# A hybrid attention and expert block on one core: the queries' and keys' projections moved ahead of the linear attention's

## The chip, the cores and the metric

The kernel runs as one launch on one core of a Trainium2 chip. The metric is the device time of the launch in microseconds. Before the change it is 1333.85 us, the median of three runs (1331.14 to 1338.91). The engines are TensorE (PE, its weight loads as PEld), VectorE (DVE), ScalarE (ACT), GpSimd (POOL) and SyncE (SP), which only issues DMAs here.

## The reference, cut to what matters

The block works on 1024 tokens of width 1024.

```
proj = h @ w_in
aq, ak, av, iq, ik, iw, bq, bk, bv, br, bg = split(proj)
aq, ak, iq, ik = rope(...)                      # rotary embedding
ya = dsa_mixer(aq, ak, av, iq, ik, iw)          # 8 heads of 64; each query sees the 256
                                                # admitted keys with the best index score
yb = gla_mixer(bq, bk, bv, log_a)               # gated linear attention, 4 heads, chunks of 64
yb = rms_norm(yb) * g_gla_norm * silu(br)
h  = layer_norm(alpha * h + concat(ya, yb) @ w_out)
y  = layer_norm(alpha * h + hier_moe(h))        # 32 experts, 2 for each token
```

In `dsa_mixer` the index score of a query and a key is `sum over 8 heads of iw * relu(iq . ik)`, keys of later chunks are excluded, and the top 256 are taken with ties in order of index. In `gla_mixer` the decay is a cumulative sum over a chunk of `log_sigmoid(bg @ w_gla_gate + b) / 16`, and the state passes from chunk to chunk.

## The kernel before, in words

Matrix products with large weights are done in a shorter format (fp32r) with both operands split in a high and a low part, and three products are summed: high x high, low x high, high x low. `proj_t` (L214 to L224) projects 128 output columns for 512 tokens with 24 matmuls of 128x512, `proj_n` (L226 to L238) two tiles of 128 tokens for 256 columns with 48 matmuls of 128x256. The splits are a cast (L179, ACT) and a subtraction (L180, DVE or POOL).

The stages around the change, in the order of the program:

- Index queries, keys and scores, beside the values' projections. Then `rest_inputs`: the second half of the values and all six projections of the linear attention (`gla_inputs`, L498: for each of two head pairs hp, k=0 the queries and keys, k=1 the values, k=2 the gate). All of it goes to DRAM.
- `queries_keys` (L657): four weight blocks of 256 columns, each projected for both halves of the tokens; rope is four DVE products from PSUM (L264 to L267) and two POOL sums (L268, L269); the result is split (ACT L179, POOL L180) and written to `d_q` and `d_k` in DRAM.
- `topk_phase` (L676): for each of six tiles of 128 queries the threshold of the 256 best is found by bisection over the bits of the score. In each of 31 bits DVE counts four tiles (L689) and ACT two (L719, by an accumulated Sign), and small DVE instructions on 128x2 or 128x4 turn counts into the next candidate (L715, L722, L723). Then come the masks, tile by tile (L738 to L750): `gt` (above the threshold, DVE L743), `eq` (equal, DVE L744), the count of `gt` (ACT L745), a running count of `eq` (DVE scan L746), the number still needed (L747), the ties taken (L748), a POOL sum (L749) and the additive bias (L750), which lies over the scores.
- `gla_phase` (L523): the linear attention in four halves (2 head pairs x 2 halves of the tokens, `gla_half`, L540), under high priority.
- `attention` (L776): 4 head pairs x 8 tiles of queries = 32 items, in three steps a turn apart: scores (L795, PE), the maximum (L800, DVE) and the exponential (L808, ACT); the transposes (L819) and their copies (L822 DVE, L824 ACT); the product with the values (`mixed`, L833). After every fourth item of a pair the reciprocal of the sums is spread by POOL (`rb`, L878), transposed into `pt` (L841), multiplied into `R` (L843) and stored in `d_mix` (`shares`). The order of PE, ACT and DVE in this stage is as written; POOL and SP are not part of that.
- `before(n)` (L334) is called ahead of item n. It loads the operands of the next pairs; at n = 8 it closes the pool `first_qk` of the first pair's operands, and in the place that is free then opens the pools of the split output weights, `wlo` and `whi` (1024x1024 each); from there on 16 pieces of w_out are loaded (`woraw`, two buffers, L901) and split by POOL into `wohi` (L908) and `wolo` (L909).
- `out_phase`: the mixed heads come back from `d_mix` into `mraw`, which has the two buffers of `woraw` (one tag, L977, L979); they are split, and multiplied by `wohi` and `wolo` (L997). Then layer norm, routing, and the 32 experts.

Outside the attention the order is the tile scheduler's: it goes by program order and priority, and an instruction that writes a buffer waits for the last readers of what lay there before. Of PSUM the linear attention has two banks (`g`) and the projections six (`acc`), all given up before the attention's (`s` two double ones, `pt` two, `ot` two) are opened.

Of the kernel before, what the change touches and what calls it, by code (L numbers as in the profile page):

```python
# [8 lines left out]
F32 = mybir.dt.float32  # L9
# [10 lines left out]
T = 1024  # L20
D = 1024
# [78 lines left out]
def const_block():  # L100
# [17 lines left out]
    add("tri", causal / 16.0)  # L118
# [10 lines left out]
NCONST = CONST_COLS["tri"][0]  # L129
# [34 lines left out]
class Kern:  # L164
# [85 lines left out]
    def banks(self, ctx, name, **tags):  # L250

        pool = ctx.enter_context(self.pool(name, space=PSUM))
        for t, n in tags.items():
            self.kinds[t] = (pool, n)

    def bank(self, kind, shape):
        pool, n = self.kinds[kind]
        return pool.tile(shape, F32, name=kind, bufs=n)
# [24 lines left out]
    def run(self):  # L283
        tc, nc, I = self.tc, self.nc, self.I
        with ExitStack() as ctx:
# [28 lines left out]
            with ExitStack() as ps:  # L314
                self.banks(ps, "psg", g=2)
                with ExitStack() as p1:
                    self.banks(p1, "ps1", acc=6)
                    self.in_phase(gla)
            self.rp = ctx.enter_context(self.pool("route"))
            with ExitStack() as ps:  # L320
                self.banks(ps, "ps2", s=2, pt=2, ot=2)
                gla.close()
                oc = outc.enter_context(self.pool("outc"))
                with self.pool("att") as ap:

                    first = ExitStack()
                    fq = first.enter_context(self.pool("first_qk", side="right"))
                    loads = [self.attention_loads(0, [fq.tile([128, 2, D], F32R, name=f"kq{i}") for i in range(3)] + [self.big()])]
# [5 lines left out]
                    def before(n):  # L334
# [31 lines left out]
    def in_phase(self, gla):  # L366
        tc, nc, I = self.tc, self.nc, self.I
        with ExitStack() as ctx:
# [6 lines left out]
            with self.pool("first") as fp:  # L375
                cI = fp.tile([128, T], F32, name="cI")
                sI = fp.tile([128, T], F32, name="sI")
                with self.pool("xraw") as xr:
# [14 lines left out]
                    K2 = self.wpool.tile([128, NCONST2], F32, name="Kin")  # L393
                    nc.sync.dma_start(K2, I["const"][:, NCONST:])
                    self.c.update({n: K2[:, a - NCONST:b - NCONST] for n, (a, b) in CONST_COLS.items() if a >= NCONST})
                    nc.gpsimd.tensor_copy(self.ones, self.c["ones"])
                    nc.gpsimd.tensor_copy(self.before, self.c["before"])
# [100 lines left out]
    def gla_inputs(self, gg):  # L498

        nc, I = self.nc, self.I  # L500
        for hp in range(2):
            w = self.load_w(I["wi"][P_GLA + 3 * hp], 256)
# [6 lines left out]
            w = self.load_w(I["wi"][P_GLA + 3 * hp + 1], 256)  # L509
# [5 lines left out]
            w = self.load_w(I["wi"][P_GLA + 3 * hp + 2], 256)  # L515
# [7 lines left out]
    def gla_phase(self, p):  # L523
# [6 lines left out]
        causal = p.tile([128, 128], I32, name="causal")  # L530
        nc.vector.tensor_copy(causal, self.c["causal"])
# [8 lines left out]
    def gla_half(self, p, hp, h, S, wg, AT, causal):  # L540
# [25 lines left out]
        for i in range(4):  # L566
            nc.tensor.matmul(bp[:, 128 * i:128 * i + 128], loga[:, 128 * i:128 * i + 128], self.c["tri"],
# [3 lines left out]
        nc.scalar.activation(eb, bp, AF.Exp)  # L571
        nc.scalar.activation(en, bp, AF.Exp, scale=-1.0)
# [57 lines left out]
        for hd in range(2):  # L630
            ss = p.tile([128, 4], F32, name="ss", bufs=2)
            sq = p.tile([128, 128], F32, name="sq")
# [43 lines left out]
    def topk_phase(self, p):  # L676
# [3 lines left out]
        gtt = p.tile([128, T], BF, name="gt", bufs=1)  # L680
        jnk = p.tile([128, T], BF, name="jnk", bufs=1)
# [55 lines left out]
        nc.vector.tensor_mul(v, thr.bitcast(F32), sg)  # L737
        for i in range(n):  # L738
            W = WS[i]
            gt = p.tile([128, T], BF, name="gt", bufs=1)[:, :W]  # L740
            eq = p.tile([128, T], BF, name="eq", bufs=1)[:, :W]
            pre = p.tile([128, T], F16, name="pre", bufs=1)[:, :W]
            nc.vector.tensor_scalar(gt, y[i], sg[:, i:i + 1], v[:, i:i + 1], op0=OP.mult, op1=OP.is_gt)  # L743
            nc.vector.tensor_scalar(eq, y[i], sg[:, i:i + 1], v[:, i:i + 1], op0=OP.mult, op1=OP.is_equal)  # L744
            nc.scalar.activation(jnk[:, :W], gt, AF.Copy, accum_out=cnt[:, i:i + 1])  # L745
            nc.vector.tensor_tensor_scan(pre, eq, eq, 0.0, op0=OP.add, op1=OP.max)  # L746
            nc.vector.tensor_scalar(need[:, i:i + 1], cnt[:, i:i + 1], -1.0, float(TOPK), op0=OP.mult, op1=OP.add)  # L747
# [3 lines left out]
        nc.vector.memset(self.bias[1][:, 0:128], 0.0)  # L751
        nc.vector.tensor_copy(self.bias[0], self.c["diag"])
        nc.vector.tensor_copy(self.bias[1][:, 128:256], self.c["diag"])
# [22 lines left out]
    def attention(self, p, before):  # L776
# [60 lines left out]
        def shares(s):  # L837
# [4 lines left out]
            R = p.tile([128, 4, 128], F32, name="R", bufs=2)  # L842
# [5 lines left out]
        with self.tc.manual_schedule(engines={mybir.EngineType.PE, mybir.EngineType.Activation, mybir.EngineType.DVE}):  # L848
            for n in range(len(items) + 2):
# [7 lines left out]
                if turn is not None:  # L857
# [3 lines left out]
                    s["ot"] = ot  # L861
                for hd in range(2):
# [11 lines left out]
                if done:  # L874
                    rb = done["rb"] = p.tile([128, 8, 64], F32, name="rb", bufs=2)
                    rr = p.tile([128, 8], F32, name="rr", bufs=2)
                    nc.vector.reciprocal(rr, done["rec"].rearrange("p a b -> p (a b)"))
                    nc.gpsimd.tensor_copy(rb, rr.unsqueeze(2).to_broadcast([128, 8, 64]))  # L878
# [605 lines left out]
```

## Time and profile before

| | us |
|---|---|
| three runs, median | 1333.85 (1331.14, 1333.85, 1338.91) |
| the profiled execution's own time | 1337.13 |
| its span | 1335.3 |
| PE busy in it | 1226.0 (92%) |
| DVE busy | 1036.9 (78%) |
| ACT busy | 803.2 (60%) |
| POOL busy | 396.5 (30%) |

The profiled execution lies 3.28 us above the median of the runs. Its span of 1335.3 us runs from the first to the last instruction, and 1.8 us lie around it. The stages in that span: projections and scores with the bisection and the first three halves of the linear attention up to 331.5, masks and the fourth half up to 394.4, the last projections of queries and keys up to 416, the first head pair from 430.6 to 456.1, the other three up to 558.8, the output projection and routing up to about 693, and then the experts.

### The profile page before, as it was taken

The numbers are of one execution on the slowest core, as the hardware profiler recorded it, in microseconds if no ns is written. First come the engines' busy times: TensorE is split into PE (matmuls) and PEld (weight loads), VectorE is DVE, ScalarE is ACT, GpSimd is POOL, SyncE is SP. The second block draws the span as 40 slices with busy tenths as digits, with TensorE's granted clock in tenths as the row PEclk, the third lists the DMA queues.
The fourth block names the chain that finished last, engine by engine and source line by source line (L and its number), as shares of the span: only waits on it lengthen the run. The fifth ranks groups of instructions, "written<-read, shape, count | busy, mean of one in ns | idle before, by whom it ended". The sixth has DMA issues, their size and how long they took to land. (4 is left out here: it accounts for less than half of the span.)

```text
span 1335.3 us, 19298 instructions
## 1 busy us (share of the span) xinstructions
PE 1226.0 (92%) x6894; PEld 1019.1 (76%) x6894; DVE 1036.9 (78%) x1640; ACT 803.2 (60%) x1119; POOL 396.5 (30%) x348
## 2 busy tenths in 40 slices
PE   6999999999896999999949999999999999999961
PEld 5987988987674778778847888888888888888841
DVE  5378799899892556467676899999999999999945
ACT  4366577676321656422135777877777777777735
POOL 2413633134763245011150122122122222123104
PEclk9998999899887999999968999999999999999985
DMA  7643334223325793397365999999999999999926
GB/s 251 169 125 113 120 97 134 88 82 109 102 64 175 224 258 107 107 324 271 119 233 200 364 368 377 377 376 363 368 367 361 362 361 348 350 361 345 331 43 248
DMA packets 127652, 318.51 MB, mean 239 GB/s; under 512 B 15353, under 2 KB 45842, under 8 KB 127554
## 3 DMA queue, kind: packets, MB, share of 16 engines
q1 hardware_dynamic: 114754, 287.86, 60.9%
q0 software_dynamic: 10496, 21.00, 6.1%
q10 hardware_dynamic: 2304, 8.39, 1.6%
q8 instruction: 55, 0.90, 0.3%
q14 instruction: 43, 0.35, 0.1%
HBM read 281.74 MB, written 52.23 MB: 250 GB/s over the span
## 5 line engine op out<-in xcount | busy, mean ns | idle before, releaser
L180 DVE TENSOR_TENSOR elo<-big,ehi 128x2048 fp32r<-128x2048 f32 (+2 forms) x136 | 270.6, 2020 | 23.3 <-ACT ehi L179 22.0
L179 ACT CAST ehi<-big 128x2048 fp32r<-128x2048 f32 (+2 forms) x136 | 225.1, 1692 | 5.9 <-DMA big<-wf 2.8
L1210 PE MATMUL acc<-ehi,xh 128*128 128x512 f32 x512 | 206.2, 403 | 2.1 <-ACT sg L1322 2.1
L1210 PE MATMUL acc<-elo,xh 128*128 128x512 f32 x512 | 203.2, 397 | 0.3 <-DVE elo L180 0.3
L1210 PE MATMUL acc<-ehi,xl 128*128 128x512 f32 x512 | 203.2, 397 | 0.0
L221 PE MATMUL acc<-big,whi 128*128 128x512 f32 (+1 forms) x432 | 139.0, 402 | 10.2 <-ACT big L179 10.0
L1280 POOL DMA_INDIRECT xg<-d_h,tok x32 | 36.9, 1153 | 368.4 <-PE pt L1273 366.3
L235 PE MATMUL acc<-whi,big 128*128 128x256 f32 x640 | 121.5, 288 | 0.0
L1259 POOL DMA_INDIRECT d_y<-y,tok x32 | 89.4, 2792 | 105.5 <-DVE y L1258 45.3
L1210 PEld LDWEIGHTS acc<-ehi,xh 128*128 128x128 f32 x512 | 97.2, 190 | 24.1 <-ACT sg L1322 2.5
L1210 PEld LDWEIGHTS acc<-ehi,xl 128*128 128x128 f32 x512 | 97.0, 189 | 23.1 <-DVE xl L180 0.2
L1210 PEld LDWEIGHTS acc<-elo,xh 128*128 128x128 f32 x512 | 97.2, 190 | 22.1 <-DVE elo L180 0.7
L221 PEld LDWEIGHTS acc<-big,whi 128*128 128x128 f32 x432 | 83.7, 198 | 28.6 <-ACT big L179 10.0
L1210 PE MATMUL ot<-ehi,ah 128*128 128x512 f32 x256 | 104.3, 407 | 0.8 <-ACT ah L179 0.8
L235 PEld LDWEIGHTS acc<-whi,big 128*128 128x128 f32 x640 | 101.9, 194 | 1.8 <-issue 1.0
L180 DVE TENSOR_TENSOR elo<-slot,ehi 128x2048 fp32r<-128x2048 f32 (+1 forms) x46 | 95.5, 2102 | 9.5 <-ACT ehi L179 7.9
L689 DVE TENSOR_SCALAR_CACHE_REDUCE gt<-sc,cand 128x384 bf16<-128x384 f32 (+1 forms) x124 | 100.5, 810 | 2.9 <-POOL sc L701 0.3
L1210 PE MATMUL ot<-ehi,al 128*128 128x512 f32 x256 | 101.8, 398 | 0.8 <-DVE al L180 0.8
L1210 PE MATMUL ot<-elo,ah 128*128 128x512 f32 x256 | 101.4, 396 | 0.0
L235 PE MATMUL acc<-wlo,big 128*128 128x256 f32 x320 | 92.5, 289 | 0.0
L719 ACT ACTIVATE jnk<-sc,cand 128x896 bf16<-128x896 f32 (+1 forms) x62 | 67.9, 1095 | 37.5 <-DVE cand L715 28.9
L221 PE MATMUL acc<-big,wlo 128*128 128x512 f32 (+1 forms) x216 | 85.8, 397 | 0.0
(286 smaller groups left out, 2633.6 us busy)
## 6 DMA issues: line engine op xcount, KB each, us to landing
big<-we SPq DMA_DIRECT2D x79, 1024.0 KB
big<-wf SPq DMA_DIRECT2D x40, 1024.0 KB
slot<-we SPq DMA_DIRECT2D x26, 1024.0 KB
sc<-we SPq DMA_DIRECT2D x20, 1024.0 KB
slot<-wf SPq DMA_DIRECT2D x16, 1024.0 KB
wraw<-wi SPq DMA_DIRECT2D x52, 256.0 KB
sc<-wf SPq DMA_DIRECT2D x8, 1024.0 KB
raw<-xT SPq DMA_DIRECT2D x8, 512.0 KB
```

Of the source, the lines that this page charges most:

```text
L179: nc.scalar.copy(hi, src)
L180: (lo_eng or nc.vector).tensor_tensor(lo, src, hi.bitcast(F32), op=OP.subtract)
L221: nc.tensor.matmul(ps[:m, :n], l[:, j, c0:c0 + m], r[:, j % 2, t0:t0 + n], start=(j == 0 and a == 0), stop=(j == 7 and a == 2))
L235: nc.tensor.matmul(ps[:, i, :], l[:, j % 2, s], r[:, j, :], start=(j == 0 and a == 0), stop=(j == 7 and a == 2))
L689: nc.vector.tensor_scalar(gtt[:, :WS[i]], x, v, 0.0, op0=op, op1=OP.add, accum_out=cnt[:, i:i + 1])
L719: nc.scalar.activation(jnk[:, :WS[i]], y[i], AF.Sign, bias=c, accum_out=cnt[:, i:i + 1])
L1210: nc.tensor.matmul(o, x[:, jj, :], w[:, j, s], start=(jj == 0 and a == 0), stop=(jj == n - 1 and a == 2))
L1259: nc.gpsimd.indirect_dma_start(out=self.d_y, out_offset=bass.IndirectOffsetOnAxis(ap=tok.bitcast(U32), axis=0), in_=y, in_offset=None, bou ...
L1280: self.last_gather = nc.gpsimd.indirect_dma_start(out=xg, out_offset=None, in_=self.d_h, in_offset=bass.IndirectOffsetOnAxis(ap=tok.bitcas ...
```

## The change: what it does

Eight edits, which belong together:

1. `queries_keys` and `topk_phase` come right after the first of the six projections of the linear attention; the other five come behind them in program order, and `gla_phase` follows with its high priority.
2. The loads of the first head pair (`attention_loads(0)`) are issued inside `in_phase`, right after `queries_keys`, into a pool `first_qk` on the right side, which now holds four tiles (with the values `kq3`; before, three and a `big` buffer). The values of `kq3` serve head pairs 0 and 1.
3. The pool of the linear attention and its two PSUM banks `g` live on, until n = 8; the attention begins with one bank of `pt` and one of `ot`, and gets the second of each at n = 8.
4. The masks: ACT takes `sn` = Sign(sg * y + v) with its sum (v negated), in place of DVE's `gt` and of ACT's counting copy; `eq` is `sn` = 0; the number needed is worked out of the sum of signs and the last value of the scan, with one more small DVE instruction.
5. The bias constants of tiles 0 and 1 are written early by POOL and not by DVE after the masks.
6. The matrix `tri` (causal / 16) is dropped; `causal` takes its place and the 1/16 goes into the scale of Exp.
7. `R` and `rb` have one buffer and not two.
8. The reciprocal and `rb` are made in the turn of the item that completes the sums, one turn earlier.

```diff
-            with self.pool("qk") as p, self.pool("topk", side="right") as tp:
-                self.queries_keys(p)
+            with self.pool("topk") as tp:
+                with self.pool("qk") as p:
+                    self.queries_keys(p)
+                fq = first.enter_context(self.pool("first_qk", side="right"))
+                loads = [self.attention_loads(0, [fq.tile([128, 2, D], F32R if i < 3 else F32, name=f"kq{i}") for i in range(4)])]
                 self.topk_phase(tp)
-            with tc.high_priority():
-                self.gla_phase(gp)
+                for hp, k in ((0, 1), (0, 2), (1, 0), (1, 1), (1, 2)):
+                    self.all_of(self.gla_inputs(gg, hp, k))
+                with tc.high_priority():
+                    self.gla_phase(gp)
+            return loads
...
-        yield from self.gla_inputs(gg)
+        yield from self.gla_inputs(gg, 0, 0)
...
-                self.banks(ps, "ps2", s=2, pt=2, ot=2)
-                gla.close()
+                self.banks(ps, "ps2", s=2, pt=1, ot=1)
...
                         if n == 8:
                             first.close()
+                            gla.close()
+                            gb.close()
+                            self.banks(ps, "ps2b", side="right", more=True, pt=1, ot=1)
...
-            gt = p.tile([128, T], BF, name="gt", bufs=1)[:, :W]
+            sn = p.tile([128, T], BF, name="sn", bufs=1)[:, :W]
...
-            nc.vector.tensor_scalar(gt, y[i], sg[:, i:i + 1], v[:, i:i + 1], op0=OP.mult, op1=OP.is_gt)
-            nc.vector.tensor_scalar(eq, y[i], sg[:, i:i + 1], v[:, i:i + 1], op0=OP.mult, op1=OP.is_equal)
-            nc.scalar.activation(jnk[:, :W], gt, AF.Copy, accum_out=cnt[:, i:i + 1])
+            nc.scalar.activation(sn, y[i], AF.Sign, scale=sg[:, i:i + 1], bias=v[:, i:i + 1], accum_out=cnt[:, i:i + 1])
+            nc.vector.tensor_scalar(eq, sn, 0.0, None, op0=OP.is_equal)
             nc.vector.tensor_tensor_scan(pre, eq, eq, 0.0, op0=OP.add, op1=OP.max)
...
-            nc.gpsimd.tensor_tensor(gt, gt, eq, op=OP.add)
-            nc.vector.tensor_scalar(self.bias[i + 2], gt, -1.0, -NEG, op0=OP.add, op1=OP.mult)
+            nc.gpsimd.tensor_tensor(sn, sn, eq, op=OP.add)
+            nc.vector.tensor_scalar(self.bias[i + 2], sn, 0.0, NEG, op0=OP.is_le, op1=OP.mult)
...
-            R = p.tile([128, 4, 128], F32, name="R", bufs=2)
+            R = p.tile([128, 4, 128], F32, name="R", bufs=1)
...
+                    if s["t"] % 4 == 3:
+                        rb = s["rb"] = p.tile([128, 8, 64], F32, name="rb", bufs=1)
...
-                if done:
-                    rb = done["rb"] = p.tile([128, 8, 64], F32, name="rb", bufs=2)
```

What this moves, on three engines. First PE, around the first scores of the attention (L795 before, L809 after; `s` is the scores' bank, `kq` the first pair's operands, `acc` the projections' bank, `g` the linear attention's, `pt` the transposes'). Before:

```order
L221 MATMUL acc<-big,wlo 128x512
L795 MATMUL s<-kq_4359,kq_4358 128x256 x2
L795 MATMUL s<-kq_4360,kq_4358 128x256 x2
L795 MATMUL s<-kq_4359,kq_4358 128x256 x2
L819 MATMUL pt<-K,Sm 128x128
L795 MATMUL s<-kq_4360,kq_4358 128x256 x2
```

And after, at the same place:

```order
L643 MATMUL g<-S,qg 64x128 x4
L234 MATMUL acc<-whi,big 128x256 x2
L234 MATMUL acc<-wlo,big 128x256
L234 MATMUL acc<-whi,big 128x256
L809 MATMUL s<-kq_2048,kq_2047 128x256 x2
L809 MATMUL s<-kq_2049,kq_2047 128x256 x2
L657 MATMUL g<-K,y 128x128 x8
L570 MATMUL g<-wg,bgT 128x128 x4
L809 MATMUL s<-kq_2048,kq_2047 128x256 x2
L833 MATMUL pt<-K,Sm 128x128
```

The projection ahead of the first scores is now that of the gate of the linear attention (`proj_n`) and not that of the last keys; behind the first item's scores stand the end of the third half of the linear attention (`g<-K,y`) and the start of the fourth (`g<-wg,bgT`). The fourth half's matmuls stand among the first head pair's items, whose transposes go by the single `pt` bank.

Next POOL, at the splitting of w_out (`woraw` its raw pieces, `wohi` and `wolo` its parts, `rb` the spread reciprocals). Before, from the first `rb` on:

```order
L878 COPY rb<-rr 128x512
L901 DMA woraw<-wo 128x512 x2
L908 CAST wohi<-woraw 128x512 x2
L909 TENSOR_TENSOR wolo<-woraw,wohi 128x512 x2
L901 DMA woraw<-wo 128x512
L878 COPY rb<-rr 128x512
L901 DMA woraw<-wo 128x512
L908 CAST wohi<-woraw 128x512 x2
```

After, from the second `rb` on:

```order
L915 DMA woraw<-wo 128x512 x2
L880 COPY rb<-rr 128x512 x3
L922 CAST wohi<-woraw 128x512 x2
L923 TENSOR_TENSOR wolo<-woraw,wohi 128x512 x2
L915 DMA woraw<-wo 128x512
L880 COPY rb<-rr 128x512
```

And after, from the eighth and last `rb` on:

```order
L880 COPY rb<-rr 128x512
L923 TENSOR_TENSOR wolo<-woraw,wohi 128x512
L915 DMA woraw<-wo 128x512 x2
L922 CAST wohi<-woraw 128x512 x2
L923 TENSOR_TENSOR wolo<-woraw,wohi 128x512 x2
L915 DMA woraw<-wo 128x512 x2
L922 CAST wohi<-woraw 128x512 x2
L923 TENSOR_TENSOR wolo<-woraw,wohi 128x512 x2
```

Before, the first two pieces are split between the first and the second `rb`, and all sixteen ahead of the seventh. Now the first cast stands behind the fourth `rb`. It writes the place of `first_qk`, whose last reader is now `mixed` of item 15 (it reads `kq3`); before, the pool held no values, and its last readers were the scores of item 7. Between the fourth and the eighth `rb` lie the splits of pieces 1 to 11 and the cast of 12; the rest of piece 12 and all of 13 to 16 come behind the eighth.

Last SP, at the end of the attention (`d_mix<-R` the stores of the mixed heads, `mraw` their loads for the output projection, `x` the residual, `big<-we` weights of the experts). Before:

```order
L845 DMA d_mix_65<-R 128x4x128
L979 DMA mraw<-d_mix_65 128x512 x2
L845 DMA d_mix_66<-R 128x4x128
L981 DMA x<-xn 128x1024
L927 DMA big<-we 128x2x1024
```

After:

```order
L859 DMA d_mix_65<-R 128x4x128
L859 DMA d_mix_66<-R 128x4x128
L995 DMA x<-xn 128x1024
L941 DMA big<-we 128x2x1024
L995 DMA x<-xn 128x1024
L941 DMA big<-we 128x2x1024 x2
L993 DMA mraw<-d_mix_65 128x512 x6
```

The first loads of `mraw` moved from ahead of the last store to behind it and behind two loads of `x` and three of expert weights; they wait for the last two pieces of w_out to leave the shared buffers.

## Rows read from the trace of the kernel before

**Rows 1.** The page: each engine's busy us, share of the span, instructions

```profile
PE 1226.0 (92%) x6894; PEld 1019.1 (76%) x6894; DVE 1036.9 (78%) x1640; ACT 803.2 (60%) x1119; POOL 396.5 (30%) x348
```

**Rows 2.** Windows: from:to, length, busy us of each engine, granted clock, DMA share, GB/s

```profile
136.00:331.50 195.50, 192.22 (x1374) 170.59 (x1373) 175.28 (x514) 136.61 (x263) 73.34 (x64) 0.98 0.33 105
331.50:394.40 62.90, 55.44 (x270) 43.22 (x269) 58.06 (x63) 19.08 (x47) 44.86 (x34) 0.89 0.26 83
394.40:416.00 21.60, 21.50 (x98) 17.22 (x96) 7.22 (x16) 3.35 (x6) 12.12 (x11) 1.00 0.44 123
416.00:430.60 14.60, 1.68 (x4) 0.89 (x4) 3.92 (x13) 1.63 (x4) 5.00 (x4) 0.61 0.62 193
430.60:456.10 25.50, 24.60 (x189) 20.09 (x189) 16.38 (x42) 17.63 (x40) 2.03 (x3) 0.89 0.67 211
456.10:491.30 35.20, 30.76 (x274) 25.08 (x272) 18.50 (x48) 20.03 (x47) 15.82 (x21) 0.95 0.93 250
491.30:521.20 29.90, 28.90 (x275) 24.11 (x273) 18.50 (x48) 20.08 (x47) 16.79 (x23) 1.00 0.65 180
```

**Rows 3.** Timeline of PE, first scores: start, us, engine, line, operation, [idle before]

```profile
430.60 0.98 PE L795 MATMUL s<-kq,kq 128*128 128x256 f32 x3 [8.97 <-DMA kq<-d_k]
```

**Rows 4.** Windows of the tile g on PE: from:to, length, busy us, granted clock

```profile
136.00:331.50 195.50, 45.34 (x372) 0.98 0.33 105
331.50:394.40 62.90, 12.41 (x100) 0.89 0.26 83
```

**Rows 5.** Groups of DVE, 131 to 332: busy us, mean ns, idle before

```profile
L715 DVE TENSOR_SCALAR cand<-thr 128x4 int32<-128x4 int32 (+1 forms) x60 | 19.0, 319 | 0.9
L723 DVE COPY_PREDICATED thr<-m,cand 128x4 int32<-128x4 int32 (+1 forms) x62 | 18.2, 296 | 0.3
L722 DVE TENSOR_TENSOR m<-cnt,need 128x4 int32<-128x4 f32 (+1 forms) x62 | 13.6, 220 | 9.2 <-ACT jnk L719 8.9
L617 DVE SCALAR_TENSOR_TENSOR S<-S,dec,kv 128x128 f32<-128x128 f32 x21 | 9.8, 469 | 2.1 <-PE g L628 1.9
```

**Rows 6.** Timeline of DVE: the small instructions alone, then beside POOL

```profile
207.79 0.17 DVE L723 COPY_PREDICATED thr<-m,cand 128x4 int32<-128x4 int32 x1
144.84 1.30 DVE L723 COPY_PREDICATED thr<-m,cand 128x4 int32<-128x4 int32 x1
146.16 1.22 DVE L715 TENSOR_SCALAR cand<-thr 128x4 int32<-128x4 int32 x1
```

**Rows 7.** Timeline of POOL beside them

```profile
144.81 3.79 POOL L180 TENSOR_TENSOR wlo<-wraw,whi 128x512 fp32r<-128x512 f32 x3
```

**Rows 8.** Groups of POOL by form, 131 to 394.4

```profile
L180 POOL TENSOR_TENSOR rp<-rp,so_hi 128x512 fp32r<-128x512 f32 x10 | 14.0, 1404 | 3.8 <-ACT so_hi L179 3.8
```

**Rows 9.** Groups of DVE by form, 331.5 to 394.4

```profile
L617 DVE SCALAR_TENSOR_TENSOR S<-S,dec,kv 128x128 f32<-128x128 f32 x7 | 7.5, 1069 | 0.2
L746 DVE TENSOR_TENSOR_SCAN pre<-eq 128x768 f16<-128x768 bf16 x1 | 2.8, 2814 | 0.0
L743 DVE TENSOR_SCALAR gt<-sc,sg,v 128x768 bf16<-128x768 f32 x1 | 1.6, 1641 | 0.0
```

**Rows 10.** Timeline of POOL: two pairs of w_out's pieces, a spread reciprocal

```profile
511.97 0.62 POOL L908 CAST wohi<-woraw 128x512 fp32r<-128x512 f32 x1 [1.20 <-DMA woraw<-wo]
513.32 2.50 POOL L909 TENSOR_TENSOR wolo<-woraw,wohi 128x512 fp32r<-128x512 f32 x2
519.08 0.61 POOL L908 CAST wohi<-woraw 128x512 fp32r<-128x512 f32 x1 [2.20 <-DMA woraw<-wo]
527.50 0.61 POOL L878 COPY rb<-rr 128x512 f32<-128x512 f32 x1 [4.27 <-DVE rr L877]
```

**Rows 11.** Timeline of PE: product of item 15, end of the attention, first output matmul

```profile
496.65 1.97 PE L833 MATMUL ot<-PT,big 128*64 128x128 f32 x32
558.84 0.50 PE L997 MATMUL acc<-wohi,m 128*128 128x512 f32 x1 [1.19 <-ACT m L179]
```

**Rows 12.** The line of the woraw DMAs: issue to landing

```profile
DMA to landing us min/median/max: 3.0/6.0/7.6
```

More of the change, by code (lines that the diff above doesn't have):

```diff
@@ L128 @@
 const_block()
-NCONST = CONST_COLS["tri"][0]
+NCONST = CONST_COLS["causal"][0]
 NCONST2 = max(b for _, b in CONST_COLS.values()) - NCONST
@@ L314, in run @@
             with ExitStack() as ps:
-                self.banks(ps, "psg", g=2)
+                gb, first = ExitStack(), ExitStack()
+                self.banks(gb, "psg", side="right", g=2)
                 with ExitStack() as p1:
                     self.banks(p1, "ps1", acc=6)
-                    self.in_phase(gla)
-            self.rp = ctx.enter_context(self.pool("route"))
-            with ExitStack() as ps:
-                self.banks(ps, "ps2", s=2, pt=2, ot=2)
-                gla.close()
+                    loads = self.in_phase(gla, first)
+                self.rp = ctx.enter_context(self.pool("route"))
+                self.banks(ps, "ps2", s=2, pt=1, ot=1)
                 oc = outc.enter_context(self.pool("outc"))
                 with self.pool("att") as ap:
-                    first = ExitStack()
-                    fq = first.enter_context(self.pool("first_qk", side="right"))
-                    loads = [self.attention_loads(0, [fq.tile([128, 2, D], F32R, name=f"kq{i}") for i in range(3)] + [self.big()])]
                     def more():
@@ L392, in in_phase @@
                     nc.sync.dma_start(self.K, I["const"][:, :NCONST])
-                    K2 = self.wpool.tile([128, NCONST2], F32, name="Kin")
+                    K2 = fp.tile([128, NCONST2], F32, name="Kin")
                     nc.sync.dma_start(K2, I["const"][:, NCONST:])
-                    self.c.update({n: K2[:, a - NCONST:b - NCONST] for n, (a, b) in CONST_COLS.items() if a >= NCONST})
-                    nc.gpsimd.tensor_copy(self.ones, self.c["ones"])
-                    nc.gpsimd.tensor_copy(self.before, self.c["before"])
+                    c = {n: K2[:, a - NCONST:b - NCONST] for n, (a, b) in CONST_COLS.items() if a >= NCONST}
+                    nc.gpsimd.tensor_copy(self.ones, c["ones"])
+                    nc.gpsimd.tensor_copy(self.before, c["before"])
+                    nc.gpsimd.memset(self.bias[1][:, 0:128], 0.0)
+                    nc.gpsimd.tensor_copy(self.bias[0], c["diag"])
+                    nc.gpsimd.tensor_copy(self.bias[1][:, 128:256], c["diag"])
                     nc.sync.dma_start(gg, I["gg"].to_broadcast([128, 128]))
@@ L496, in rstd, with gla_inputs @@
         self.last_pow = nc.gpsimd.tensor_tensor(out, out, self.mhalf[:, :n], op=OP.pow)
[L498 removed]
+    def gla_inputs(self, gg, hp, k):
         nc, I = self.nc, self.I
[L501 to L502 removed]
+        w = self.load_w(I["wi"][P_GLA + 3 * hp + k], 256)
+        if k == 0:
             for h in range(2):
@@ L566, in gla_half @@
         for i in range(4):
-            nc.tensor.matmul(bp[:, 128 * i:128 * i + 128], loga[:, 128 * i:128 * i + 128], self.c["tri"],
+            nc.tensor.matmul(bp[:, 128 * i:128 * i + 128], loga[:, 128 * i:128 * i + 128], self.c["causal"],
                              start=True, stop=True)
```

45 lines of the change are left out of this document (23 added, 22 removed).

## The prediction

> **What bounds the kernel now.** I read the page first [rows 1]: PE is busy for 1226.0 of 1335.3 us, so only the stretches in which it is not can give much. Windows by stage show them [rows 2]. The projections up to 331.5 run at 192.22 busy us of 195.5. Beside the masks, 331.5 to 394.4, PE is busy 55.44 of 62.9 at a granted clock of 0.89; DVE, at 58.06, is the full engine there. From 416.0 to 430.6 PE has next to nothing (1.68 of 14.6): the timeline shows the first scores waiting for the first pair's keys, the last 8.97 us up to 430.60, released by a DMA that reads `d_k` [rows 3]. After that stall the first pair runs at 0.89 [rows 2]: 25.5 x 0.11 = 2.8 us. The second pair takes 35.2 us where the third takes 29.9 [rows 2]; the third is full (28.90 of 29.9). So the idle PE is about 8 + 13 + 4 us, and lost clock about 10 (0.11 of 62.9, 2.8 behind the stall). Whether DVE lets that be had is the question.
>
> **A. Start of the attention, from 430.6 to about 392.** Two engines bound it.
>
> By PE: projections end at 416.0 [rows 2]. The fourth half of the linear attention moves behind the first scores. The tile `g` takes 45.34 + 12.41 us on PE in all four halves [rows 4], 14.4 each; pipelined tails overlap the neighbours, so I take 12. 416.0 - 12 = 404. The 7.5 idle us beside the masks [rows 2] should go, since the projections are then not bound to ropes that queue behind masks, and 62.9 x 0.09 = 5.7 us of clock with them: 404 - 13 = 391. If neither comes back it is 404.
>
> By DVE: from 136 to 416 it is busy 175.28 + 58.06 + 7.22 = 240.6 us [rows 2]. `gt` leaves it (six of up to 1.64, 6 us by the row of 768 columns scaled [rows 9]); the fourth half leaves it, 8.5 us by estimate (S alone took 7.5 there [rows 9], by its mean elsewhere of 0.469 it takes 3.3 [rows 5], and a few products and copies go with it: 6 to 11); six tiny instructions come, each 0.17 alone and up to 1.30 [rows 6], 1 to 8 us, of which I take 2. 240.6 - 6 - 8.5 + 2 = 228. Its idle time from 136 to 331.5 is 20.2 us and 4.8 to 394.4 [rows 2]; 136 + 228 + 25 = 389. The rope products, 32 in both kernels, only stand earlier.
>
> The masks themselves stay a chain. Sign on ACT, `eq`, scan (2.8 at the widest row [rows 9]), need, taken, the POOL sum and the bias pass one single buffer each, so six tiles are serial. Moving `gt` to ACT takes work from DVE and no link from the chain; I cost it at nothing beyond the 6 us, from -6 to +6.
>
> What the earlier ropes do to the bisection is the open term. Alone, L723 takes 0.17 us; beside a POOL subtraction it and L715 took 1.30 and 1.22 [rows 6, 7]. Over the bisection the means of L715, L723 and L722 are 0.319, 0.296 and 0.220 [rows 5]; less 0.17 each, over 60, 62 and 62 of them, that is 8.9 + 7.8 + 3.1 = 20 us of being held, beside 73.34 us of POOL [rows 2], 0.27 us for each us of POOL. Of eight rope sets, four POOL instructions of 1.4 us each [rows 8], about six move from the masks into the bisection: 6 x 4 x 1.4 = 34 us, times 0.27 = 9 us. They stop blocking the masks, where S took 1.07 and not 0.47 us [rows 5, 9]. I set one against the other: zero, from -5 to +20 (24 instructions moved, one small DVE instruction held by each for 1.2 us, is 29, less the 9 already likely to be given back).
>
> So about 392 by either engine, with 380 (idle DVE time shrinks too) and 412 as ends. The 14.6 us stall is covered: the first pair's DMAs go out before the masks. **-38.6 us** (-51 to -19).
>
> **B. First pair, 25.5 to about 42.** PE is busy 24.6 there at a clock of 0.89 [rows 2]; at full clock 22, and the fourth half's 12 is added: 34. `pt` and `ot` have one bank each up to item 8, ACT has its 17.6 us [rows 2] plus a half's own, and the first items' maxima wait behind the third half's DVE work. PE was idle 4.4 us in the second pair and 7.5 beside the masks, where the fourth half's chain stood [rows 2]. I take 8, near the latter, from 3 (where each fills the other's gaps) to 14 (both and a little). **+16.5** (+11.5 to +22.5). Of A, then, 12 us come back here; the rest of A is idle time and clock.
>
> **C. Second pair, 35.2 to 30.2.** Its loads go out earlier, and w_out is not split in it (POOL 15.82 us of it [rows 2]). It should take what the third takes, 29.9. **-5** (-5.3 to 0).
>
> **D. Output projection behind w_out.** Before, seven of the eight pairs of pieces are under way by 519.08 [rows 10]. In the new order the first cast waits for the product of item 15, which ended at 498.6 (496.65 + 1.97 [rows 11]); call that zero. The output projection began at 558.84 [rows 11], 60.2 later. The third pair shows 29.9 / 8 = 3.74 us an item [rows 2]; the last `rb` of POOL belongs to item 31 and is made in the turn in which its transposes are, 15 turns after item 15's product; less the part of a turn by which the exponential precedes the end of the turn's product (some 3.5, about one item), that is 52.5. Behind it stand half of the twelfth piece and pieces 13 to 16. Two pieces with nothing in between took 7.1 us from cast to cast (511.97 to 519.08), and the second ends 3.85 after its first cast (513.32 + 2.50 less 511.97) [rows 10]. So: 52.5 + 1.3 = 53.8, first cast of 13 some 3.5 later at 57.3, of 15 at 64.5, done at 68.4. Only then may `mraw` be read, since the two buffers are shared, and SP has loads of `x` and of expert weights ahead of it: 5 us to landing (3.0 to 7.6, by the pieces of the same size [rows 12]) and 1.2 for the cast that PE waits for [rows 11]: 74.6, 14.4 later than before (10 to 19 by these ends). PE has nothing else, so its clock falls as it did behind the stall at 416 (0.61, then 0.89 [rows 2]): another 2.8, from 1 (a shorter stall) to 5. **+17.5** (+11 to +24). If the splits were hidden, this term would be zero.
>
> The early `rr` and `rb`, the single `R`, the dropped `tri` and the biases written early I cost at nothing: `rb` had 4.27 us of POOL waiting for `rr` [rows 10], so POOL is not late; a single `R` waits for a store that has four items, 15 us, to land.
>
> Sum: -38.6 + 16.5 - 5 + 17.5 = -9.6. Against the profiled execution's own 1337.13 that is 1327.5; it lay 3.28 above the median of the runs, so **1324.3 us** is what I expect of a median.
>
> The Trainium skill has a rule on the open term. SBUF — State Buffer, "SBUF: two separate sides", says that VectorE and GpSimd share a port pair as an exclusive lock: one that has it keeps it for a whole instruction while the other stands still, for VectorE instructions in a two-port mode or with two SBUF inputs. The rows of 1.30 and 1.22 us beside a POOL subtraction agree, and by that rule the earlier ropes hold the bisection, which is the first rival.
>
> **Rivals.**
>
> 1. *The bisection is held by POOL (slower).* Place: L715, L722 and L723 between the first and last bit, with the moved ropes on POOL. Price: 29 us in the bisection with 9 given back in the masks, +20: first scores flow at 412, -18.6 + 16.5 - 5 + 17.5 = +10.4, a median of 1344. It decides from the point at which A brings less than 22.3 us, so first scores after 408, for then the sum is over +6.7. For it: counts are in a serial chain with those instructions, 31 times. Against: POOL's load of 73 us there already costs only 20.
>
> 2. *The splits are not late.* If POOL's last `rb` came early enough, or `mraw` found its buffers free, D goes: -27.1, a median of 1307. For it: before, the seventh pair was cast at 519.08 [rows 10], some 40 us ahead of its use. Against: the order puts four pieces behind the last `rb`, and two pairs at 7.1 us don't fit into the 7.7 that are left (60.2 - 52.5).
>
> 3. *First pair crowded.* Single `pt`, a half's chain on DVE and ACT, few banks: B is 27 and not 16.5, a median of 1335, no change. For it: DVE is full up to the last mask, and the first maximum stands behind the third half's products. Against: DVE was busy only 16.38 of the first pair's 25.5 us [rows 2].
>
> **How the numbers follow.** No change means within 0.5%, 6.7 us, about what a measurement of this kernel can tell: 1327.2 to 1340.5. Chances: the forecast 0.52 (its own range 1314 to 1334; faster in two thirds of it), rival 1 0.20 (slower in two thirds, the rest no change), rival 2 0.10 (faster), rival 3 0.18 (no change in two thirds, slower in a quarter). Faster: 0.35 + 0.10 + 0.02 = 0.47. Slower: 0.13 + 0.05 = 0.18. No change: 0.35. The range leaves out the best of rival 2 and the worst of rival 1: 1307 to 1344.
>
> **What would show it.** A: the first scores at 385 to 400, with no wait on the keys' DMA, and the last mask shortly after; means of L715 and L723 near 0.35 us (rival 1: 0.45 or more). B: the first pair at 42 us with matmuls of `g` in it and PE waits of some 8 us. C: 30 us. D: first `wohi` cast right behind item 15's product, an idle PE of 12 to 20 us before the first output matmul, ended by ACT's cast of `m` and before that by the DMA into `mraw`, and a clock below 1 after it. The forecast is wrong if the output projection begins without a wait, or if the attention starts after 408.

## The result and the profile after

The changed kernel takes 1367.77 us (median of four runs, 1365.64 to 1373.1), the kernel before beside it 1332.49: a ratio of 1.0259, with a 95% interval of 1.0233 to 1.0284. The forecast was 1324 in a range of 1307 to 1344. The change makes the kernel 35 us slower, and the way it fails is none of the three rivals as they were put.

The profiled execution after took 1365.64 us with a span of 1363.9, 28.6 more than the span of before. The page's row that answers to [rows 1] shows hardly more work on any engine (ACT 2.2 us), and less on PE, DVE and POOL:

```profile
PE 1219.5 (89%) x6894; PEld 1016.4 (75%) x6894; DVE 1017.0 (75%) x1636; ACT 805.4 (59%) x1119; POOL 393.8 (29%) x351
```

The time is in waits. Windows of the changed kernel (columns as in [rows 2]; the cuts lie where its own stages begin):

```profile
136.00:253.00 117.00, 117.00 (x614) 100.18 (x614) 103.85 (x264) 59.28 (x102) 71.19 (x55) 1.00 0.34 115
253.00:278.00 25.00, 0.75 (x12) 0.58 (x15) 18.92 (x61) 11.84 (x21) 4.46 (x4) 0.60 0.54 171
278.00:351.40 73.40, 71.52 (x489) 63.47 (x483) 56.16 (x173) 52.22 (x100) 25.92 (x23) 0.93 0.49 148
351.40:394.40 43.00, 41.29 (x355) 38.73 (x354) 28.57 (x54) 21.12 (x45) 15.36 (x14) 1.00 0.19 63
394.40:412.80 18.40, 18.40 (x162) 15.47 (x163) 4.51 (x11) 2.73 (x6) 4.48 (x3) 1.00 0.44 128
412.80:422.50 9.70, 4.87 (x23) 3.71 (x21) 3.24 (x21) 5.72 (x21) 3.63 (x5) 0.62 1.06 282
422.50:433.00 10.50, 4.78 (x19) 3.13 (x18) 3.70 (x12) 5.80 (x11) 1.27 (x1) 0.50 1.07 310
433.00:473.40 40.40, 34.29 (x291) 26.37 (x287) 21.20 (x51) 22.25 (x57) 6.32 (x10) 0.97 0.46 136
473.40:512.50 39.10, 36.26 (x361) 30.50 (x360) 21.57 (x59) 23.35 (x57) 1.69 (x4) 1.00 0.25 69
572.00:589.30 17.30, 0.04 (x1) 0.04 (x1) 0.74 (x2) 0.75 (x2) 7.78 (x9) 0.60 0.86 319
```

Three rows stand out: 25 us from 253 with no PE work, 20 us from 412.8 with PE half idle at a granted clock of 0.62 and 0.50, and 17 us from 572 with none again. The timeline of PE names what ended each wait (in brackets: idle us before, and the releaser):

```profile
277.70 1.99 PE L616 MATMUL g<-v,kd 64*64 64x128 f32 x32 [24.25 <-DMA v<-d_gv]
412.84 0.63 PE L809 MATMUL s<-kq,kq 128*128 128x256 f32 x4
417.60 1.08 PE L657 MATMUL g<-K,y 128*128 128x128 f32 x4 [4.13 <-DVE y L653]
431.97 0.69 PE L833 MATMUL pt<-K,Sm 128*128 128x128 f32 x2 [5.64 <-ACT PT L838]
589.26 0.80 PE L1011 MATMUL acc<-wohi,m 128*128 128x512 f32 x1 [17.79 <-ACT m L178]
```

Before, the first scores flowed at 430.60 behind a wait of 8.97 [rows 3]; now they start at 412.84 without one, but a wait of 24.25 us lies 135 us ahead of them. The spans put against before, by the prediction's parts:

| part | before | after | measured | forecast |
|---|---|---|---|---|
| A, first scores flow | 430.6 | 412.8 | -17.8 | -38.6 |
| B, first pair | 25.5 | 60.6 | +35.1 | +16.5 |
| C, from there to the end of item 15's product | 42.5 | 39.0 | -3.5 | -5 |
| D, from there to the output projection | 60.2 | 76.9 | +16.7 | +17.5 |
| behind it | 776.5 | 774.6 | -1.9 | in D |
| sum (spans) | | | +28.6 | -9.6 |

The end of item 15's product (C and D) is the start at 510.43 plus 1.97 in the trace after. The forecast of D has 2.8 us in it for a lower clock behind its wait, in a stage that came out 1.9 us shorter. D came near its forecast; A and B are each some 20 us off.

### The profile page after: what moved, and what is told of

Same layout as the page of the kernel before. It is cut to its first block, busy times and chain, and to the rows that moved or that the text cites. A ratio compares the mean times of both kernels' runs of the same rounds, so it can differ in the third digit from the quotient of the medians.

```text
span 1363.9 us, 19283 instructions
## 1 busy us (share of the span) xinstructions
PE 1219.5 (89%) x6894; PEld 1016.4 (75%) x6894; DVE 1017.0 (75%) x1636; ACT 805.4 (59%) x1119; POOL 393.8 (29%) x351
## 5 line engine op out<-in xcount | busy, mean ns | idle before, releaser
L220 PE MATMUL acc<-big,whi 128*128 128x512 f32 (+1 forms) x432 | 134.6, 391 | 11.9 <-ACT big L178 10.9
L704 DVE TENSOR_SCALAR_CACHE_REDUCE eq<-sc,cand 128x384 bf16<-128x384 f32 (+1 forms) x124 | 100.3, 809 | 4.7 <-POOL sc L716 2.3
L1011 PE MATMUL acc<-wohi,m 128*128 128x512 f32 x256 | 84.2, 406 | 17.8 <-ACT m L178 17.8
L734 ACT ACTIVATE sn<-sc,cand 128x896 bf16<-128x896 f32 (+1 forms) x62 | 67.9, 1095 | 42.6 <-DVE cand L730 22.0
```

The lines of the kernel that those rows point to most:

```text
L220: nc.tensor.matmul(ps[:m, :n], l[:, j, c0:c0 + m], r[:, j % 2, t0:t0 + n], start=(j == 0 and a == 0), stop=(j == 7 and a == 2))
L704: nc.vector.tensor_scalar(gtt[:, :WS[i]], x, v, 0.0, op0=op, op1=OP.add, accum_out=cnt[:, i:i + 1])
L734: nc.scalar.activation(jnk[:, :WS[i]], y[i], AF.Sign, bias=c, accum_out=cnt[:, i:i + 1])
L1011: nc.tensor.matmul(ps, l[:, j, :], w[:, j, s], start=(j == 0 and a == 0), stop=(j == 7 and a == 2))
```

## Experiments

In all of them the kernel before ran beside, at medians of 1332.7 to 1333.9.

**The values ahead.** Theory W is that PE's wait at 253 is its own loss; theory B is my first rival.

```diff
         yield from self.gla_inputs(gg, 0, 0)
+        yield from self.gla_inputs(gg, 0, 1)
...
-                for hp, k in ((0, 1), (0, 2), (1, 0), (1, 1), (1, 2)):
+                for hp, k in ((0, 2), (1, 0), (1, 1), (1, 2)):
```

> Edit: of the linear attention's projections also the first pair's values (0,1) go ahead of the queries' and keys'. Theory W (PE's wait for the values): the wait of 24.25 us for v goes, first scores come at 386 to 392 in place of 412.8, and the median falls by 22 to 27 us from 1367.8, to about 1343; the first pair stays at about 60 us and the wait behind w_out at 17 us. Theory B (my first rival, the bisection held by POOL): the wait only covered a late DVE, first scores stay behind 405 and the median falls by less than 8 us.

Measured: 1371.82, no gain. The wait for `v` went, and one as long came 35 us later. The timelines of PE and of DVE in this kernel:

```profile
312.97 1.08 PE L658 MATMUL g<-K,y 128*128 128x128 f32 x4 [25.24 <-DVE y L654]
311.70 1.13 DVE L654 SCALAR_TENSOR_TENSOR y<-g,ss,gs 128x128 f32<-128x128 f32 x4 [8.94 <-DMA gs<-d_gr]
```

`y` is DVE's, but DVE waited for `gs`, the gate, which was now the first thing of that head pair to be projected behind the queries and keys. W missed. B's two numbers came true (first scores at 418.65, no fall), but not its reason: what DVE waited for there was a load (8.94 us) and not POOL. What W and B had in common, that one wait is to be taken away, was the error.

**The loads behind.** Does SP's queue make the wait? In the changed kernel SP did this (start, us, line, operation):

```profile
263.72 0.34 SPq L526 DMA_DIRECT2D d_gv<-vs  x1
264.16 0.38 SPq L779 DMA_DIRECT2D kq<-d_q  x1
272.41 0.33 SPq L782 DMA_DIRECT2D kq<-d_k  x1
273.01 0.33 SPq L564 DMA_DIRECT2D v<-d_gv  x1
```

The values' store is issued at 263.72, the load of `v` only at 273.01, behind a load of keys that waited for the keys' last store.

```diff
-                loads = [self.attention_loads(0, [fq.tile([128, 2, D], F32R if i < 3 else F32, name=f"kq{i}") for i in range(4)])]
                 self.topk_phase(tp)
                 for hp, k in ((0, 1), (0, 2), (1, 0), (1, 1), (1, 2)):
                     self.all_of(self.gla_inputs(gg, hp, k))
+                loads = [self.attention_loads(0, [fq.tile([128, 2, D], F32R if i < 3 else F32, name=f"kq{i}") for i in range(4)])]
```

> Edit: the first pair's loads are issued behind the linear attention's projections in program order, so that the load of v does not stand behind a load of kq that waited 7.8 us for the keys' last store. Theory W1 (SP's queue makes the wait for v long): the wait falls from 24.25 to 16 to 18 us and the median by 5 to 8 us. Theory W2 (the path of v itself: ACT copy, store, load): the wait falls by less than 3 us, the median by less than 3.

Measured: 1368.57, and the wait was 25.28 us. But the edit moved the loads in the program and not in SP's order, so the run tests neither W1 nor W2. In this run SP did the same as in the changed kernel:

```profile
264.99 0.38 SPq L779 DMA_DIRECT2D kq<-d_q  x1
273.23 0.33 SPq L782 DMA_DIRECT2D kq<-d_k  x1
273.84 0.33 SPq L564 DMA_DIRECT2D v<-d_gv  x1
```

The trace of the changed kernel tells more. Between 250 and 282 SP waited for these stores (us in total, times, longest), and ACT did the following around the copy of the values:

```profile
SPq L782 <- DMA d_k<-rp: 7.8, 1, 7.8
SPq L564 <- DMA d_gv<-vs: 0.2, 1, 0.2
255.39 0.62 ACT L178 CAST whi<-wraw 128x512 fp32r<-128x512 f32 x1 [4.78 <-DMA wraw<-wi]
263.13 0.56 ACT L525 COPY vs<-acc 128x512 f32<-128x512 f32 x1
```

When the keys' load had gone out, SP still had to wait 0.2 us for the values' own store. So the load of `v` could not have left earlier, and the place in the queue cost it next to nothing here, as W2 has it. The wait of 24.25 us is the path itself: ACT's copy came 9.7 us after PE had stopped (277.70 - 24.25 = 253.45), the store landed some 9 us after its issue, and PE began 4.7 us after the load was issued. ACT's copy stood behind a cast that waited for weights and behind counts of the bisection. What made the copy late and the store slow was not tried apart.

**The first head pair's projections all ahead.**

```diff
-        yield from self.gla_inputs(gg, 0, 0)
+        for k in range(3):
+            yield from self.gla_inputs(gg, 0, k)
...
-                for hp, k in ((0, 1), (0, 2), (1, 0), (1, 1), (1, 2)):
+                for hp, k in ((1, 0), (1, 1), (1, 2)):
```

> Edit: all three projections of the linear attention's first head pair go ahead of the queries' and keys'; only the second pair's stay behind. Theory W (PE, in a fixed order, waits for what has to go through DRAM: with the values alone moved, the wait went over to the gate, 25.24 us ahead of the transposes of y): with values and gate early no wait of over 5 us is left up to the first scores, these come at 386 to 394, and the median falls by 18 to 27 us from 1367.8. Theory M (the order holds another such wait, now of the second pair's values or gate): one wait of 10 us or more stands between 300 and 412, first scores stay behind 402, the median falls by less than 12. Theory B (DVE held): no wait of PE on a DMA is left, but one on DVE or ACT takes its place, first scores behind 405.

Measured: 1360.04. Theory M: the wait moved again, to the third half, 19.87 us, and the first scores came at 411.8. PE's and DVE's timelines:

```profile
351.10 1.11 PE L598 MATMUL g<-K,kdT 128*128 128x128 f32 x4 [19.87 <-POOL kdT L594]
349.23 0.69 DVE L590 TENSOR_TENSOR kg<-kg,en 128x512 f32<-128x512 f32 x1 [3.98 <-DMA kg<-d_gqk]
```

PE waits for POOL, POOL for DVE, DVE for `kg`, which is what (1, 0) projects: again the first projection behind the queries' and keys'.

**All five projections ahead.**

```diff
-        yield from self.gla_inputs(gg, 0, 0)
+        for hp in range(2):
+            for k in range(3):
+                yield from self.gla_inputs(gg, hp, k)
...
-                for hp, k in ((0, 1), (0, 2), (1, 0), (1, 1), (1, 2)):
-                    self.all_of(self.gla_inputs(gg, hp, k))
```

> Edit: all five projections go back ahead of the queries' and keys', the rest of the change stays (the first pair's operands in the right-side pool, one pt and ot bank up to item 8, Sign masks). Theory W' (a half whose inputs are projected behind the queries' and keys' makes PE wait for their way through DRAM; moved twice, the wait came back each time): no wait of PE of over 5 us before the end of the projections, which end at 402 to 412; the fourth half is then under projections again, the first pair takes 25 to 30 us in place of 60.6; ahead of it the wait for the first pair's keys is back, 8 to 16 us. First item of the second pair at 444 to 456 in place of 473.4, and with the wait behind w_out unchanged (17 us) the median falls by 17 to 29 us, to 1339 to 1351. If the single pt bank made the first pair long, it stays over 40 us.

Measured: 1386.49, the slowest of all. The part on the halves held: no wait of PE over 2.6 us up to 415.3, and the fourth half was back under the projections. The first pair took 34.9 us (456.7 to 491.6), so one bank of `pt` alone does not make it long. But the wait for the keys was 41.41 us where I expected 8 to 16:

```profile
456.67 0.55 PE L809 MATMUL s<-kq,kq 128*128 128x256 f32 x1 [41.41 <-DMA kq<-d_k]
```

In this order SP issued the second pair's loads (from 419.69) ahead of the first's (445.48), and the first pair's keys had to wait for the last store of `d_k`, issued at 439.16. Which of the two made the wait so long is open.

**Only the last gate behind**, and the second head pair with its own values (the edit of the next experiment).

> Edit: of the linear attention's projections only the second pair's gate stays behind the queries' and keys' (23 us of PE work for the first pair's loads to hide under), and the second head pair loads its own values. Theory W': the gate is wanted only at the end of the third half, behind the last projection, so no wait over 5 us before it; first scores at 394 to 404; the fourth half stands beside the first pair, which takes 50 to 60 us; the median is 1325 to 1342. If the gate's way through DRAM holds the start: a wait of 10 us or more for y right behind the first scores.

Measured: 1358.39. The wait did not come for `y`, as I thought it might, but in front of the first scores, released by a store of that gate:

```profile
417.76 1.22 PE L810 MATMUL s<-kq,kq 128*128 128x256 f32 x4 [23.76 <-DMA d_gr<-vs]
410.24 1.62 SPq L534 DMA_DIRECT2D d_gr<-vs  x2
```

SP issued that store at 410.24, behind the first pair's loads in its queue (390.79 to 408.20), one of which waited 8.1 us for the keys' last store; ACT needed the store to get a buffer back before it could copy the rest of the gate out of PSUM, and the scores waited for that. Here, other than for `v`, the place in SP's queue did make the wait.

So in each of the orders tried one wait of 20 to 45 us stands ahead of the first scores. This case's kernel before has 14.6 us there (1.68 of them busy, [rows 2]), and that is the smallest of them.

**The second pair's own values** (for D). The place of `first_qk` is then free after item 7 and not item 15.

```diff
-                        loads.append(self.attention_loads(hp, [self.big(F32R) for _ in range(3)] + ([self.big()] if hp == 2 else [])))
+                        loads.append(self.attention_loads(hp, [self.big(F32R) for _ in range(3)] + ([self.big()] if hp < 3 else [])))
...
-        if hp % 2 == 0:
+        if hp < 3:
             self.vv = slots[3]
...
-            if hp % 2 == 0:
+            if hp < 3:
                 nc.sync.dma_start(self.vv.rearrange("p a (t c) -> p a t c", c=128)[:, :, 4 * th:4 * th + 4],
```

> Edit: the second head pair loads its own copy of the values (1 MB more of DMA), so the place of the first pair's operands is free after item 7's product and not item 15's. Theory D (the splits of w_out wait for that place and hold the output projection): the first cast comes within 10 us of the second pair's start, the 17 us without PE work ahead of the output projection go, and the median falls by 14 to 18 us, to about 1352. Rival: the splits in the second pair and the extra load cost what is won (before, the second pair took 42.4 us up to item 15's product, now 39.1): the median falls by less than 8 us.

Measured: 1343.36, 24.4 less than the changed kernel, for 1 MB more of DMA; its ratio to the kernel before is 1.0087 (1.0058 to 1.0116). The first cast comes at 474.05, item 15's product ends at 505.7, and the output projection starts 60.3 us behind it, as it did before (60.2):

```profile
474.05 1.18 POOL L922 CAST wohi<-woraw 128x512 fp32r<-128x512 f32 x2 [6.89 <-PE ot L847]
565.98 0.50 PE L1011 MATMUL acc<-wohi,m 128*128 128x512 f32 x1 [1.24 <-ACT m L178]
```

The rest is a start 2.7 us earlier and a first pair of 56.5 us (410.15 to 466.68): the wait of 5.64 us for `PT` is 1.48 there, since ACT's order no longer has a copy of `ym` at that place.

**Both.** The first head pair's three projections ahead, with own values.

> Edit: the last one together with the second head pair's own copy of the values (which alone gave 1343.4). Theory W: the two gains add, 1318 to 1326, below the kernel before. If the waits stand one for the other: 1335 to 1345.

Measured: 1343.07. The 8 us that the first edit brought do not add to the 24; its wait of 20.26 us for `kdT` stayed. **All five ahead with own values:**

> Edit: the last one, and the second head pair loads its own values. Theory W' and D: the gains add, so that also the 17 us ahead of the output projection go: 1321 to 1333, no slower than the kernel before. If not additive: 1335 to 1345.

Measured: 1372.42; D's gain is there (14 us on 1386.49), the wait for the keys is 45.03.

**The half ahead of the attention** (for B).

```diff
-                self.banks(ps, "ps2", s=2, pt=1, ot=1)
+                gb.close()
+                self.banks(ps, "ps2", s=2, pt=2, ot=2)
...
-                            gb.close()
-                            self.banks(ps, "ps2b", side="right", more=True, pt=1, ot=1)
```

> Edit: the linear attention's two PSUM banks are closed ahead of the attention, which has two pt and two ot banks from the start, so the fourth half ends before the first transposes get their second bank. Theory P (crowding: the half beside the first pair costs more than its 12 us, through one pt bank, ACT's order and half the clock): scores start 12 to 16 us later, at 425 to 430, the first pair falls from 60.6 to 26 to 34 us, and the median falls by 12 to 20 us. Theory Q (the half costs its own work wherever it stands): the first pair falls by what the start loses, median within 4 us of 1367.8.

Measured: 1376.74, 9 us slower than the changed kernel. Theory P had the pair right (28.4) and fell on the median, and Q fell too: with nothing beside it, what is left of the linear attention takes 47.6 us, of which PE works 23.33 at a granted clock of 0.55. Windows of this kernel:

```profile
413.00:460.60 47.60, 23.33 (x134) 17.57 (x133) 11.66 (x38) 15.62 (x44) 9.04 (x12) 0.55 0.75 213
460.60:489.00 28.40, 26.61 (x200) 21.91 (x200) 16.90 (x46) 19.01 (x44) 2.03 (x3) 0.85 0.16 47
```

And of PE's timeline the two longest waits in it:

```profile
433.46 2.08 PE L580 MATMUL g<-causal,loga 128*128 128x128 f32 x8 [10.73 <-POOL loga L577]
438.77 1.12 PE L596 MATMUL g<-K,kdT 128*128 128x128 f32 x4 [3.23 <-POOL kdT L592]
```

A half is a chain through PE, DVE, ACT and POOL. Overlapping it with the first pair saves 15 us (47.6 + 28.4 against 60.6), but its length is near 40 and not 12.

**The second pair's loads later.** In the first pair ACT stood still for the copy of `ym`, whose buffer waited for its last store, and loaded two tables around it (start, us, line, operation):

```profile
429.13 0.59 ACT L659 COPY ym<-g 128x512 f32<-128x512 f32 x1 [3.58 <-DMA d_mix<-ym]
429.73 1.28 ACT L577 ACT_TABLE_LOAD   x1
431.03 0.63 ACT L577 ACTIVATE u<-u 128x512 f32<-128x512 f32 x1
431.56 0.35 ACT L838 COPY PT<-pt 128x256 f32<-128x256 f32 x1
431.94 1.28 ACT L822 ACT_TABLE_LOAD   x1
```

```diff
-                        if n in (0, 12, 19):
+                        if n in (3, 12, 19):
```

> Edit: the second head pair's operands are loaded from item 3 on and not from item 0. Theory S (SP's queue and the DMA engines, busy at a share of 1.05 with these loads from 412 to 433, hold the store of ym, ACT stands 3.58 us at the next copy of ym, and PE 5.64 us for the copy of PT behind it): PE's wait falls from 5.64 to below 2, the first pair by 3 to 6 us, the median by 3 to 6. Rival: the wait is ACT's own order and its table loads (1.28 us each): first pair within 2 us of 60.6.

Measured: 1370.04 (1363.81 to 1371.48), no change. The wait fell from 5.64 to 4.67 only, and the first pair is 59.5: theory S is not borne out at that size. How ACT's wait for the store divides between SP's queue and the transfers is open.

**The masks alone, in the kernel before** (the change's `sn` in place of `gt`, as in the change's diff).

> The kernel before with the masks of the change alone (Sign on ACT). I costed this part at nothing beside 6 us of DVE: the stretch of the masks, 61 us from v to the last bias, gets 0 to 8 us shorter, the median stays within 6 us of before. If the change's loss lay in the masks' chain, this kernel would be slower by more than 6 us.

Measured: 1333.91, a ratio of 1.0011 (0.9994 to 1.0029). From `v` to the last bias it takes 62.0 us (329.95 to 391.96), 61.1 before: no change, and no part of the loss.

**The earlier reciprocals alone, in the kernel before.**

```diff
+                    if s["t"] % 4 == 3:
+                        rb = s["rb"] = p.tile([128, 8, 64], F32, name="rb", bufs=2)
...
-                if done:
-                    rb = done["rb"] = p.tile([128, 8, 64], F32, name="rb", bufs=2)
```

> The kernel before with one part of the change alone: the reciprocal and rb one turn earlier (two buffers kept). I costed this part at nothing. In the second pair of the kernel before PE waits 2.32 us for rb, behind a split of w_out on POOL; if the earlier rb takes that away and nothing else moves, the second pair falls from 35.2 to about 32 and the median by 1 to 4 us below the kernel before; if POOL's order puts it behind a split all the same, the median stays within 1.5 us. In neither case does this part carry the change's loss.

Measured: 1333.47, ratio 1.0002 (0.9988 to 1.0017). The wait of 2.32 us for `rb` went, but one of 3.35 us for the copy of `R` came in its place. Neither part carries the loss. No version tried beats the kernel before.

## Why the prediction was wrong, point by point

**A failed at a term that its sum by PE put at nothing: the waits that the new order makes.** The step is "404 - 13 = 391", which takes idle time away and adds none. The 7.5 idle us beside the masks did go: PE is idle for 1.7 of the 43.0 us from 351.4, and for none of the 18.4 behind them. But a wait of 24.25 us came at 253. I asked which idle time the new order gives back and not which waits it makes. The halves' inputs go from PE over an ACT copy, a store and a load. Before, the load of the first half's values went out at 153.29 and PE used them at 173.50, and PE did other projections of the linear attention all the time between (columns as in [rows 2]):

```profile
153.29:173.50 20.21, 20.21 (x165) 19.54 (x164) 16.63 (x48) 16.09 (x26) 9.11 (x8) 1.00 0.49 148
```

In the new order the half stands in PE's fixed order right behind the projection that feeds it. When the values, or all of the first head pair, were moved ahead, the wait came back with the first projection left behind; with only the last gate left, it stood ahead of the first scores, by way of that gate's store; with none left, the scores waited for their keys. By subtraction the rest of the sum was right: 412.8 - 24.25 = 388.6, where I had 389 and 391. No run shows it, as the earliest first scores of any are at 410.15. The trace of before showed a trip of this kind, 8.97 us at the end of a 14.6 us wait for `kq`; I used it only as something that the change removes.

**B failed at its 12 us, and the 8 of waiting with them.** I took the half's busy time on PE for its cost where its cover was gone. By the half set ahead, what is left of the chain is 47.6 us; beside the pair it costs 25.7 over the 34.9 that the pair takes with one `pt` bank and no half (order put back). By estimate some 4 of these at most go to the clock, granted at 0.62 and 0.50 from 412.8 to 433, since PE was busy for only half of that time (4.87 x 0.38 + 4.78 x 0.50). Rival 3 named the right place and one right reason, the half's chain on DVE and ACT, and put B at 27 us where it measured 35.1; its other reason, few banks, is at most the 6.5 us between 34.9 and the 28.4 with two.

**C** came at -3.5 for -5.

**D was right in mechanism, and its total nearly so.** The wait was put at 14.4 us and measured 16.7. Of the clock's 2.8 us, put on top of it (which makes 17.2 and not 17.5), 1.6 came by estimate: the granted clock was 0.85 from 589.3 to 600 (10.7 x 0.15), where the same stage before had 1.00. First cast at 512.48, behind item 15's product (512.40); the eighth `rb` 53.4 us behind that, forecast 52.5. POOL after, at the end:

```profile
512.48 1.18 POOL L922 CAST wohi<-woraw 128x512 fp32r<-128x512 f32 x2 [5.84 <-PE ot L847]
565.81 0.61 POOL L880 COPY rb<-rr 128x512 f32<-128x512 f32 x1 [3.82 <-DVE rr L879]
571.12 0.61 POOL L922 CAST wohi<-woraw 128x512 fp32r<-128x512 f32 x1 [2.41 <-DMA woraw<-wo]
582.09 0.61 POOL L922 CAST wohi<-woraw 128x512 fp32r<-128x512 f32 x1 [5.10 <-DMA woraw<-wo]
584.04 2.48 POOL L923 TENSOR_TENSOR wolo<-woraw,wohi 128x512 fp32r<-128x512 f32 x2
```

The last pair came 11.0 us behind the one before it and not 7.1, with the DMA engines at a share of 0.86 by then; `mraw` was there 2 us behind the last split and not 5, so that the errors cancel in part. That part is luck.

**Rival 1** named a loss that is there, and too small. The small instructions of the bisection after (columns as in [rows 5]):

```profile
L730 DVE TENSOR_SCALAR cand<-thr 128x4 int32<-128x4 int32 (+1 forms) x60 | 22.2, 373 | 1.0
L738 DVE COPY_PREDICATED thr<-m,cand 128x4 int32<-128x4 int32 (+1 forms) x62 | 18.8, 305 | 0.3
L737 DVE TENSOR_TENSOR m<-cnt,need 128x4 int32<-128x4 f32 (+1 forms) x62 | 15.3, 249 | 13.2 <-ACT sn L734 13.0
```

Less 0.17 each they were held 12.2 + 8.4 + 4.9 = 25.5 us, for 19.8 before, beside 101.6 us of POOL for 73.3: again a quarter of a us for each, +5.7 where I set 9, and it did not bound the start, which PE did without an idle us from 394.4. The exclusive lock that the Trainium skill states (SBUF — State Buffer, "SBUF: two separate sides") agrees with these means, but no run takes POOL's work away to show the lock as their cause. The price was what the rows gave, not the 29 us of every instruction held once. The masks gave more back than I had set: 46.6 us from `v` to the last bias (351.4 to 398.0), for 61.1.

**Costed at nothing, rightly:** the masks by Sign and the earlier reciprocals, each within 0.3% alone. The single `R` and `rb`, the dropped `tri` and the early bias constants were not tried apart.

## What to carry to other kernels

Where each engine works in a fixed order, moving a block of work takes its cover away from everything that it lay over: list what waits under the block before it is moved, and price it by the length of its chain and not by its busy time on one engine. A value's way through DRAM cost PE nothing under 20 us of other work, and 20 to 25 us of standing still where its user stood right behind its projection. A load moved in the program need not move in the queue: in the run with the loads behind, SP's order stayed as it was. And a buffer takes over the last reader of what shares its pool: one tile read eight items longer cost 17 us at the end of a stage, and the run with a copy of its own won them back.

## What was not expected of the hardware

While PE stood and started again from 412.8 to 433, the granted clock was 0.62 and then 0.50, 1.2 GHz of 2.4, though PE was busy for half of that time; before, the stall of 14.6 us at 416 was followed by 0.89 over the whole pair [rows 2].
